# x and mem read a second time with features first; Strassen's sums from the kept normalised x; the first weights in two halves

## The chip, the core and the metric

The kernel runs on one core of a Trainium2 chip. The core's engines run side by side and wait for each other on semaphores: PE (matrix products; PEld is its weight load), DVE and ACT (elementwise work), POOL (here it issues DMAs and little else) and SP (issues DMAs only). The metric is the device time of one execution in microseconds (us), lower is better. A row of the trace such as `PE L143 MATMUL pg<-whi,memh 128*128 128x512 f32` names the engine, the line that recorded the operation, the operation, the tile written and the tiles read, and the shape.

## What is computed

One layer of a decoder trunk over 512 tokens with 2048 features, and 256 memory tokens. The part that the change touches is the entry:

```python
h = rms_norm(x, norm_g)                       # (512, 2048)
proj = h @ w_in                               # 13712 columns: three branches, gates
...
mkv = rms_norm(mem, mem_norm_g) @ w_mem_kv    # (256, 2048) @ (2048, 2048)
ck = rms_norm(mkv[..., :1024].reshape(..., 4, 256), c_k_norm_g)
cv = mkv[..., 1024:].reshape(..., 4, 256)
...
x = x + merged @ w_out
```

`rms_norm(x, g)` divides each token's row by the root of its mean square (plus 1e-6) and multiplies feature by feature with `g`.

## The kernel before, in words

**Products.** PE contracts over the partition axis, so each left operand must lie with features on partitions. All products are float32 made of three passes: each operand is split into a high part (ACT rounds it: `whi`, `memh`, `hh`) and a rest (DVE subtracts: `wlo`, `meml`, `hl`), and PE adds high·high, high·rest and rest·high.

**The stream.** `stream` (line 379) walks through a list of *jobs*. A job of the memory projection is one block of 256 rows by 512 columns of `w_mem_kv` (512 KB): one DMA from SP into a buffer (`wraw`, three of them, or `mraw`, four), one split on ACT, one subtraction on DVE, twelve matmuls (two halves of 128 rows, two blocks of 128 memory tokens, three passes). The projection has four *chunks* of 512 columns with eight jobs each. Chunk `iq0` follows (eight jobs of 24 matmuls), the first one that reads x, and then chunks of 1024 columns by Strassen's algorithm with seven products P1 to P7 of quarter blocks. SP loads weights as buffers come free; up to three jobs are split ahead (`LOOK`).

**The threads.** Side work (normalisation, attention, sums) is written as generators. `run` (line 628) takes steps of them between the jobs' matmuls, by a model of the engines' clocks (`Plan`, line 74) that exists only while the program is written. It settles the order of instructions on each engine; on the chip an engine goes through its own list in that order and stops only where an instruction waits for a semaphore.

**The entry.** `mem_in` is loaded token by token (`px<-mem`, five DMAs on SP between the first weights). `mem_thread` (825) calls `turn_tokens` (784): PE turns blocks of 128 by 128 with a product by the identity (`pa<-ident,px`, 32 of them), ACT and DVE scale by the gain and split from PSUM. The mean squares of mem are taken on ACT, and `mem_rs` scales the chunk's results as they leave PSUM. `x_thread` (840) starts when mem is turned (flag "mem"): eight DMAs of 512 KB on SP (`px<-x`), sums of squares on ACT, a scaling of each row on DVE, 64 turned blocks, and the split into `hh`, `hl`. `small_loads` (709) fetches 13 small tensors by DMAs from POOL; `rotary_tables` (734) follows x.

**The sums for Strassen.** `h_ops_thread` (1659) needs sums and differences of quarters of h. It adds `hh` and `hl` back together (`h_r<-hh,hl`, eight DVE instructions), makes S1, S2, S4 for two groups of features, splits each, and sets "P1 made", which lets the stream prepare the first Strassen weights.

Before the first weights arrive PE multiplies identity tiles in bf16 (`idle`, 703; `WARM = (28, 24)`).

Of the kernel before, what the change touches and what calls it, by code (L numbers as in the profile page):

```python
# [43 lines left out]
def constants():  # L44

    c = np.zeros((P, 33), np.float32)
    c[:, 0] = np.tile(np.asarray(BUCKET_START, np.float32), 4)
    c[:, 1:33] = (10000.0 ** (-np.arange(0, 64, 2) / 64)).astype(np.float32)[None]
    return c

# [226 lines left out]
class Kern:  # L277
# [101 lines left out]
    def stream(self):  # L379
# [33 lines left out]
        def load_some(most):  # L413
            while st["nload"] < len(loads) and most > 0:
# [4 lines left out]
                if l["strassen"] and "strassen pool" not in self.flags:  # L419
                    return  # L420
                pool = dict(wraw=self.wp, sraw=self.gp, so=self.bp, mraw=self.mp)[l["tag"]]
                r = pool.tile([P, 2, 512], F32, name=l["tag"], tag=l["tag"], bufs=size[l["tag"]])
                if isinstance(l["src"], tuple):
# [33 lines left out]
        def halves(jb, src, w, ids=(), now=False):  # L457
            h, l = new_pair()
            h, l = h[:, :, :w], l[:, :, :w]
            nc.scalar.activation(h, src, AF.Copy)  # L460
# [3 lines left out]
            def low():  # L464
                tt(l, src, h, op=OP.subtract)
                done(*ids)
# [4 lines left out]
        def prep(jb):  # L471
# [11 lines left out]
            elif p == "P5":  # L483
                if kb == 0:
                    sh["T2"] = self.gp.tile([P, c["kp"], 512], F32, name="T2", tag="t2")
# [32 lines left out]
        yield "boot"  # L518
# [4 lines left out]
        for ji, jb in enumerate(jobs):  # L523
# [52 lines left out]
            self.backlog = self.CLEAR if jb["last"] and "gates" in self.flags else self.BACKLOG  # L576
# [38 lines left out]
    BOOT = 3  # L615
    WARM = (28, 24)
    REST = 4
    BACKLOG = 4500.0
    CLEAR = 1500.0
    backlog = BACKLOG  # L620
# [7 lines left out]
    def run(self, main, threads):  # L628
# [38 lines left out]
        for r in main:  # L667
            if r == "boot":
                for _ in range(self.BOOT):
                    step(live[0])  # L670
            elif r == "stall":
# [10 lines left out]
    def setup(self):  # L682
# [12 lines left out]
        self.idle(self.WARM[0])  # L695
# [5 lines left out]
        nc.vector.tensor_copy(self.mnegb, self.mneg)  # L701

# [6 lines left out]
    def small_loads(self):  # L709

        nc, A, cp = self.nc, self.A, self.cp
        self.cst = cp.tile([P, 33], F32, name="cst")
        nc.gpsimd.dma_start(self.cst, A["consts"])

        def col(name, src, n):
            t = cp.tile([P, n], F32, name=name)
            nc.gpsimd.dma_start(t, src.rearrange("o (n p) -> p (o n)", p=P),)
            return t

        self.g_x = col("g_x", A["norm_g"], KT)  # L720
        self.g_aq = col("g_aq", A["a_q_norm_g"], 1)
        self.g_ak = col("g_ak", A["a_k_norm_g"], 1)
        self.g_bl = col("g_bl", A["b_q_lat_norm_g"], 4)
        self.g_bk = col("g_bk", A["b_kv_lat_norm_g"], 2)
        self.g_bqn = col("g_bqn", A["b_q_norm_g"][:, :P], 1)
        self.g_bkn = col("g_bkn", A["b_k_norm_g"][:, :P], 1)
        self.g_cq = col("g_cq", A["c_q_norm_g"], 2)
        self.g_ck = col("g_ck", A["c_k_norm_g"], 2)
        self.g_bqr = cp.tile([P, 64], F32, name="g_bqr")
        nc.gpsimd.dma_start(self.g_bqr, A["b_q_norm_g"][:, P:].to_broadcast([P, 64]))  # L730
        self.g_bkr = cp.tile([P, 64], F32, name="g_bkr")
        nc.gpsimd.dma_start(self.g_bkr, A["b_k_norm_g"][:, P:].to_broadcast([P, 64]))

    def rotary_tables(self, pool):

        nc, A, cp = self.nc, self.A, self.cp
        pos = A["positions"]
        pi = pool.tile([P, NT], I32, name="pos_i")
        nc.gpsimd.dma_start(pi, pos.rearrange("o (n p) -> p (o n)", p=P))
        pf = pool.tile([P, NT], F32, name="pos_f")  # L740
        nc.vector.tensor_copy(pf, pi)
# [23 lines left out]
        self.cos = cp.tile([P, NT, 32], F32, name="cos")  # L765
        nc.scalar.activation(self.sin, r, AF.Sin)
        nc.vector.tensor_scalar(k, r, -1.0, None, op0=OP.mult)
        nc.vector.tensor_tensor(k, r, k, op=OP.max)
        nc.vector.tensor_scalar(k, k, -1.0, math.pi / 2, op0=OP.mult, op1=OP.add)
        nc.scalar.activation(self.cos, k, AF.Sin)  # L770
# [13 lines left out]
    def turn_tokens(self, n, src, half, gain, name, boot=False):  # L784
# [3 lines left out]
        per = 4 // n  # L788
        prev = None

        def finish():
            k0, pt = prev
            ks = range(k0, k0 + per)
            ps = [pt[:, k - k0].rearrange("p a b -> p (a b)") for k in ks]
            for k, x in zip(ks, ps):
                nc.scalar.activation(half(k)[0], x, AF.Copy, scale=gain[:, k:k + 1])
            for k, x in zip(ks, ps):
                nc.vector.scalar_tensor_tensor(half(k)[1], x, gain[:, k:k + 1], half(k)[0], op0=OP.mult,
                                               op1=OP.subtract)
                self.flags.add("%s%d" % (name, k))  # L800

        for i, k0 in enumerate(range(0, KT, per)):
            ring = (self.pa, self.pb)[i % 2]
            blocks = [(k, t) + src(t, k) for k in range(k0, k0 + per) for t in range(n)]
            if boot and i > 1:
                yield "job %d" % min(i // 2, 2)
            yield [x[3] for x in blocks] + [ring]
            pt = ring.bank([P, per, n, P])
            for k, t, x, _ in blocks:
                nc.tensor.transpose(pt[:, k - k0, t], x, self.ident)  # L810
            if prev:
                yield [prev[1]]
                finish()
            prev = (k0, pt)
            if boot:
                if i == 0:
                    self.idle(self.WARM[1])
                yield [pt]
                finish()
                prev = None  # L820
        if prev:
            yield [prev[1]]
            finish()

    def mem_thread(self, pool, hi, lo):
        nc = self.nc
        xs = self.mem_in
        yield from self.turn_tokens(2, lambda t, k: (xs[k // 4][:, t, k % 4 * P:(k % 4 + 1) * P], xs[k // 4]),
                                    lambda k: (hi[:, k], lo[:, k]), self.g_m, "mem", True)
        self.flags.add("mem")  # L830
        ss = pool.tile([P, 2], F32, name="m_ss")
        v = pool.tile([P, 2], F32, name="m_v")
        for t in range(2):
            yield from self.sum_squares(pool, [x[:, t] for x in xs], ss[:, t:t + 1])
        yield
        nc.vector.tensor_scalar(v, ss, 1.0 / D, EPS, op0=OP.mult, op1=OP.add)
        self.rsqrt(pool, self.mem_rs, v, 2)
        self.flags.add("mem rs")

    def x_thread(self, pool):  # L840
        nc = self.nc
        src = self.A["x"][0]
        yield "mem"
        xs = []
# [3 lines left out]
        for t in range(NT):  # L848
            xs.append([])
            for q in range(2):  # L850
                x = pool.tile([P, 1024], F32, name="px", tag="px", bufs=8)
                nc.sync.dma_start(x, src[t * P:(t + 1) * P, q * 1024:(q + 1) * 1024])
                xs[t].append(x)
                for _ in range(self.REST):
                    yield
        self.small_loads()
        for t in range(NT):
            yield xs[t]
            yield from self.sum_squares(pool, xs[t], ss[:, t:t + 1])
        yield [ss]  # L860
        nc.vector.tensor_scalar(v, ss, 1.0 / D, EPS, op0=OP.mult, op1=OP.add)
        self.rsqrt(pool, rs, v, NT)
        for t in range(NT):
            for x in xs[t]:
                nc.vector.tensor_scalar(x, x, rs[:, t:t + 1], None, op0=OP.mult)
                yield
        yield from self.turn_tokens(NT, lambda t, k: (xs[t][k // 8][:, k % 8 * P:(k % 8 + 1) * P], xs[t][k // 8]),
                                    self.act_h, self.g_x, "x")
        self.flags.add("x")
        self.rotary_tables(pool)  # L870
# [145 lines left out]
    def c_thread(self):  # L1016
        nc = self.nc
        yield "ipool"
        with self.slots("cpool") as pool:
# [15 lines left out]
            rs_c = pool.tile([P, 4, 6], F32, name="c_rs")  # L1035
            nc.vector.tensor_scalar(vv, self.c_ss, 1.0 / 256, EPS, op0=OP.mult, op1=OP.add)
            self.rsqrt(pool, rs_c.rearrange("p a b -> p (a b)"), vv.rearrange("p a b -> p (a b)"), 24)
            nc.vector.tensor_scalar(rs_c[:, :, :4], rs_c[:, :, :4], C_SCALE, None, op0=OP.mult)
            for h in range(4):
# [34 lines left out]
                yield from self.split_in_turn(vh, vl, v)  # L1074
# [584 lines left out]
    def h_ops_thread(self):  # L1659
# [4 lines left out]
        yield "strassen pool"  # L1664
# [5 lines left out]
        for g in range(2):  # L1670
            ks = slice(4 * g, 4 * g + 4)
            r = self.gp.tile([P, 4, 4, 256], F32, name="h_r", tag="t2")
            blocks = [(j, i) for j in range(2) for i in range(2)]
            for x, (j, i) in enumerate(blocks):
                hi, lo = [y[:, :, 256 * i:256 * i + 256] for y in self.h[2 * j + g]]
                tt(r[:, x], hi, lo, op=OP.add)
                yield [r]
            r11, r21, r12, r22 = [r[:, x] for x in range(4)]
# [3 lines left out]
            yield [r]  # L1682
# [625 lines left out]
```

## Time and profile before

| what | value |
|---|---|
| runs | 1845.24, 1845.20 and 1845.78 us, median 1845.24 us |
| span of the profiled execution, first to last instruction | 1844.1 us |
| between that span and the median of the runs | 1.1 us |
| PE busy | 1831.6 us in 9313 matmuls |
| DVE busy | 1379.0 us |
| ACT busy | 981.5 us |
| POOL busy | 210.0 us |
| moved by DMA | 368.55 MB, 200 GB/s on the mean |

The profile counts an engine as busy while an instruction is in it. Matmuls overlap in the array, so the time that one of them adds to a chain is read from the distance between the starts of neighbours, and not from its own duration. "x24" after a row is a count; "[1.53 <-DMA mraw<-w_mem_kv]" is an idle spell of the engine just before, and what ended it. A window's row gives the busy time of PE, PEld, DVE, ACT and POOL in it, then the granted clock of PE as a share of full speed, the busy share of the 16 DMA engines and GB/s.

### The profile page before, as it was taken

What the parts mean: (1) busy time and instruction counts of PE and PEld (TensorE: products, weight loads), DVE (VectorE), ACT (ScalarE), POOL (GpSimd) and SP (SyncE); (2) the same over time, 40 slices, a digit from 0 to 9 for tenths busy, and PEclk for the clock granted to TensorE, in tenths of its full rate; (3) what the DMA queues carried; (4) which work ended last, traced back from release to release, by engine and by line L of the source; (5) the groups of instructions that cost most, each with busy time, mean ns of one, the idle gap of its engine ahead of it and who ended that gap; (6) DMA issues with size and microseconds to landing.
All of it is one profiled execution on the core that took longest, in us unless ns stands there. A gap on an engine that the chain in (4) does not pass through costs nothing.

```text
span 1844.1 us, 25398 instructions
## 1 busy us (share of the span) xinstructions
PE 1831.6 (99%) x9313; PEld 1533.4 (83%) x9313; DVE 1379.0 (75%) x2118; ACT 981.5 (53%) x1789; POOL 210.0 (11%) x310
## 2 busy tenths in 40 slices
PE   9999999999999999999999999999999999999999
PEld 7887888888888888888889888888878888888787
DVE  6788787777777877778777588999867675667755
ACT  7734544464444444444458866545877942234442
POOL 1000011001010110000112212210112112110000
PEclk9999999999999999999999999999999999999999
DMA  9654596876667967656636634333366467846784
GB/s 344 217 190 136 166 353 186 228 207 182 201 243 254 263 182 206 195 170 194 203 127 220 215 131 137 131 121 119 112 227 210 133 221 260 285 160 206 247 276 139
DMA packets 159756, 368.55 MB, mean 200 GB/s; under 512 B 19072, under 2 KB 27184, under 8 KB 158608
## 3 DMA queue, kind: packets, MB, share of 16 engines
q1 hardware_dynamic: 120592, 232.72, 39.7%
q0 software_dynamic: 39008, 134.21, 22.5%
q8 instruction: 73, 1.20, 0.3%
q14 instruction: 51, 0.42, 0.1%
q10 hardware_dynamic: 32, 0.01, 0.0%
HBM read 308.40 MB, written 92.05 MB: 217 GB/s over the span
## 4 chain that ended last, share of the span: by engine, by line
PE 89%; DVE 6%; ACT 3%; issue 1%; DMA 1%; POOL 0%; SPq 0%; ACTq 0%; DVEq 0%
PE pg L143 55%; PE pn L143 26%; PE pm L143 8%; DVE wlo L143 1%; ACT whi L143 1%; DMA stage<-sp_oC 1%; DVE i_wk L143 1%; DVE i_mx L143 0%; ACT b_pr L143 0%; ACT junk L143 0%; DVE b_st L143 0%; DMA px<-mem 0%; ACT a_st L143 0%; PE pb L143 0%; DVE b_rl L143 0%
## 5 line engine op out<-in xcount | busy, mean ns | idle before, releaser
L143 ACT ACTIVATE whi<-wraw 128x1024 fp32r<-128x1024 f32 (+2 forms) x266 | 277.8, 1047 | 293.1 <-PE pg L143 150.7
L143 DVE TENSOR_TENSOR wlo<-wraw,whi 128x1024 fp32r<-128x1024 f32 (+2 forms) x266 | 321.3, 1209 | 141.2 <-ACT whi L143 140.0
L143 PE MATMUL pg<-whi,u 128*128 128x512 f32 x640 | 216.5, 399 | 0.0
L143 PE MATMUL pg<-hh,whi 128*128 128x512 f32 x448 | 181.7, 406 | 1.0 <-DVE stage L143 1.0
L143 ACT ACTIVATE whi<-sraw 128x1024 fp32r<-128x1024 f32 (+1 forms) x99 | 103.8, 1050 | 134.8 <-DVE sraw L143 59.5
L143 PE MATMUL pg<-hh,wlo 128*128 128x512 f32 x448 | 175.2, 391 | 0.0
L143 PE MATMUL pg<-hl,whi 128*128 128x512 f32 x448 | 174.8, 390 | 0.0
L143 DVE TENSOR_TENSOR wlo<-sraw,whi 128x1024 fp32r<-128x1024 f32 (+1 forms) x99 | 119.9, 1213 | 56.6 <-ACT whi L143 55.7
L143 PE MATMUL pg<-whi,hS 128*128 128x512 f32 (+1 forms) x480 | 156.8, 388 | 0.0
L143 PE MATMUL pn<-whi,hS 128*128 128x512 f32 (+1 forms) x480 | 156.3, 386 | 0.0
L143 PEld LDWEIGHTS pg<-whi,u 128*128 128x128 f32 x640 | 120.2, 188 | 23.2
L143 PE MATMUL pg<-wlo,u 128*128 128x512 f32 x320 | 124.9, 390 | 0.0
L143 PE MATMUL pg<-whi,hl 128*128 128x512 f32 (+1 forms) x320 | 124.0, 388 | 0.0
L143 PE MATMUL pn<-whi,hl 128*128 128x512 f32 (+1 forms) x320 | 124.0, 388 | 0.0
L143 PE MATMUL pg<-wlo,hh 128*128 128x512 f32 (+1 forms) x320 | 123.9, 387 | 0.0
L143 PE MATMUL pn<-wlo,hh 128*128 128x512 f32 (+1 forms) x320 | 123.9, 387 | 0.0
L143 PE MATMUL pn<-whi,hh 128*128 128x512 f32 (+1 forms) x320 | 123.7, 387 | 0.0
L143 PE MATMUL pg<-whi,hh 128*128 128x512 f32 (+1 forms) x320 | 123.7, 387 | 0.0
L143 DVE TENSOR_TENSOR wlo<-T,whi 128x1024 fp32r<-128x1024 f32 (+1 forms) x80 | 96.7, 1209 | 31.3 <-ACT whi L143 31.1
L143 ACT ACTIVATE whi<-T 128x1024 fp32r<-128x1024 f32 (+1 forms) x80 | 84.0, 1050 | 67.7 <-PE pn L143 25.9
L143 PEld LDWEIGHTS pg<-whi,hS 128*128 128x128 f32 x480 | 90.1, 188 | 18.0
L143 PEld LDWEIGHTS pn<-whi,hS 128*128 128x128 f32 x480 | 90.1, 188 | 17.3
(452 smaller groups left out, 4112.7 us busy)
## 6 DMA issues: line engine op xcount, KB each, us to landing
wraw<-w_in SPq DMA_DIRECT2D x146, 512.0 KB, 3.9
sraw<-w_in SPq DMA_DIRECT2D x90, 512.0 KB, 4.3
wT<-w_out POOLq DMA_DIRECT2D x24, 1024.0 KB, 21.4
wraw<-w_branch SPq DMA_DIRECT2D x48, 512.0 KB, 4.7
yg<-sp_g POOLq DMA_DIRECT2D x24, 512.0 KB, 5.3
wraw<-wT SPq DMA_DIRECT2D x19, 512.0 KB, 4.0
mraw<-w_mem_kv SPq DMA_DIRECT2D x17, 512.0 KB, 6.9
wT<-wT POOLq DMA_DIRECT2D x8, 1024.0 KB, 12.7
```

Source lines behind the costliest of these rows:

```text
L143: return f(*a, **k)
```

## The change

Two inputs more are given to the kernel, `xT` and `memT`: x and mem with features first (2048 by 512, 2048 by 256). The small parameters arrive in one array `cols` of 191 columns, and `g_m` by itself.

```diff
+    def x_loads(self):
+        nc = self.nc
+        yield "mem2"
+        src = self.A["x"][0]
+        self.rows = [self.hp[n // 2].tile([P, D], F32, name="row%d" % t, tag="h%s%d" % (x, n)) ...]
+        pieces = [("row%d %d" % (t, h), self.rows[t][:, h * 1024:(h + 1) * 1024], src[t * P:(t + 1) * P, ...])
+                  for t in range(NT) for h in range(2)]
+        pieces += [("xs%d" % k, self.xs[k // 4][:, k % 4:k % 4 + 2], self.A["xT"][k * P:(k + 2) * P]...)
+                   for k in range(0, KT, 2)]
+        for name, a, b in pieces:
+            nc.gpsimd.dma_start(a, b)
+            self.flags.add(name)
+            for _ in range(self.REST):
+                yield
...
     def mem_thread(self, pool, hi, lo):
-        yield from self.turn_tokens(2, ..., self.g_m, "mem", True)
+        for i in range(KT // 2):
+            ...
+            for k, x, g in ks:
+                nc.scalar.activation(hi[k // 2][:, k % 2], x, AF.Copy, scale=g)
+            for k, x, g in ks:
+                nc.vector.scalar_tensor_tensor(lo[k // 2][:, k % 2], x, g, hi[k // 2][:, k % 2], ...)
...
     def x_thread(self, pool):
-                nc.sync.dma_start(x, src[t * P:(t + 1) * P, q * 1024:(q + 1) * 1024])
...
-            for x in xs[t]:
-                nc.vector.tensor_scalar(x, x, rs[:, t:t + 1], None, op0=OP.mult)
-        yield from self.turn_tokens(NT, ..., self.act_h, self.g_x, "x")
+        nc.vector.tensor_copy(wide, bc(rs, [P, NT, P], 2))
+        for t in range(NT):
+            nc.tensor.transpose(pt[:, t * P:(t + 1) * P], wide[:, t], self.ident)
+        nc.scalar.activation(rb, pt, AF.Copy)
+        for i in range(KT // 2):
+            for a in range(2):
+                nc.vector.scalar_tensor_tensor(x[:, a], x[:, a], self.g_x[...], rb, op0=OP.mult, op1=OP.mult)
+            self.split(hh, hl, x)
...
     def h_ops_thread(self):
-                tt(r[:, x], hi, lo, op=OP.add)
-            r11, r21, r12, r22 = [r[:, x] for x in range(4)]
+            r11, r21, r12, r22 = [self.xs[2 * j + g][:, :, 256 * i:256 * i + 256] for j in range(2) for i in range(2)]
...
-                if g and n == "S1":
+                if g and n == "S2":
                     self.flags.add("P1 made")
+        self.more_gates()
...
         def load_some(most):
-                if l["strassen"] and "strassen pool" not in self.flags:
+                if l["tag"] == "sraw" and "strassen pool" not in self.flags:
+                if isinstance(l["src"], tuple) and not st["nload"]:
+                    (w,), row = l["src"]
+                    for k in range(2):
+                        nc.sync.dma_start(r[:, k], w[row + k * P:row + k * P + P, :])
+                        self.second_load()
...
-    WARM = (28, 24)
+    WARM = 36
+    FIRST = 8000.0
...
         def mem_load(a, b):
-            q = a // 512
-            load(self.mem_in[q][:, :, a - q * 512:b - q * 512], src[:, :, a:b])
+            q = a // 4
+            load(self.mem_in[q][:, a - 4 * q:b - 4 * q], src[:, a:b])
```

So mem comes with features on partitions, in pieces of 1, 1, 2, 2, 2, 4 and 4 feature blocks; no block of it is turned. Its squares are summed over features by ACT and DVE (`mem_stats`, new: four squares, three adds, four small products by a column of ones on PE), and `mem_rs` is now applied to the keys' norms and to the values in `c_thread`. x is read twice, by rows for its sums of squares and with features first for the work. The factor 1/rms of each token is spread over all partitions by four turned blocks (`x_rb`), and x is scaled in place and kept, which gives `h_ops_thread` its quarters. The tiles `xs` make room for the weights `sraw` only when these sums are made (`more_gates`). `rotary_tables` runs later, in the Strassen stage. The first job's weights are loaded and split in two halves.

On POOL, at the start of the program, up to the first evacuated result of the memory projection. Before (`sp_ck0` is that result, the rest are small parameters):

```order
L686 IOTA jp_90 128x128
L143 DMA sp_ck0_153<-stage_526 128x1024 [waits DVE_49,Activation_49]
L143 DMA cst_615<-consts 128x33
L143 DMA g_x_617<-norm_g 128x16x1
L143 DMA g_aq_619<-a_q_norm_g 128x1
```

And now (`row` is x by tokens, `xs` x by features; a wait named DMASW is for a DMA that POOL itself issued earlier):

```order
L711 IOTA jp_90 128x128
L157 DMA row0_260<-x 128x1024 x2
L157 DMA row1_261<-x 128x1024 x2
L157 DMA cols_303<-cols 128x191
L157 DMA row2_262<-x 128x1024 x2
L157 DMA row3_263<-x 128x1024
L157 DMA row3_263<-x 128x1024 [waits DMASW0_49]
L157 DMA xs0_160<-xT 128x2x512 [waits DMASW1_49]
L157 DMA xs0_160<-xT 128x2x512 [waits DMASW2_49]
L157 DMA sp_ck0_180<-stage_462 128x1024 [waits DMASW3_49,DVE_49,Activation_49]
```

Eight halves of x's rows and two pieces of `xs`, ten DMAs of 512 KB, stand ahead of `sp_ck0`, and none of them waits for SP, PE, ACT or DVE.

On SP, the first loads. Before (`px` is mem, `wraw` and `mraw` weights):

```order
L143 DMA px_192<-mem 128x2x256
L143 DMA wraw_198<-w_mem_kv 128x2x512
L143 DMA px_192<-mem 128x2x256
L143 DMA wraw_201<-w_mem_kv 128x2x512
L143 DMA px_193<-mem 128x2x512
L143 DMA wraw_204<-w_mem_kv 128x2x512
L143 DMA px_194<-mem 128x2x512
```

And now:

```order
L157 DMA mem0_150<-memT 128x256
L157 DMA wraw_220<-w_mem_kv 128x512
L157 DMA mem0_150<-memT 128x256
L157 DMA wraw_220<-w_mem_kv 128x512
L157 DMA mem0_150<-memT 128x2x256
L157 DMA wraw_225<-w_mem_kv 128x2x512
L157 DMA mem1_151<-memT 128x2x256
L157 DMA wraw_228<-w_mem_kv 128x2x512 [waits DMAHW0_49]
```

The same bytes in smaller first pieces; the eight loads of x that stood on SP further down have gone to POOL.

On DVE, at the end of `iq0` and the start of the first Strassen chunk. Before (`hS` are the split sums, `stage` takes iq0's result out of PSUM, `T2` and `wraw<-wraw` are sums of weights):

```order
L143 TENSOR_TENSOR hS2_1242<-h_r_1374,hS2_1242 128x1024 [waits Activation_49]
L143 TENSOR_TENSOR h_r_1374<-h_r_1374 128x1024
L143 TENSOR_TENSOR hS4_1243<-h_r_1374,hS4_1243 128x1024 [waits Activation_49]
L143 COPY stage_1483<-pg_1216 128x512 [waits DMASW0_49,PE_49]
L143 COPY stage_1501<-pg_1218 128x512 [waits DMASW5_49,PE_49]
L143 TENSOR_TENSOR T2_1511<-wraw_1386,wraw_1316 128x1024 [waits DMAHW0_49,DVE_49]
L143 TENSOR_TENSOR wraw_1349<-wraw_1386,wraw_1349 128x1024
L143 TENSOR_TENSOR wlo_1514<-wraw_1316,whi_1513 128x1024 [waits Activation_49]
```

And now:

```order
L157 TENSOR_TENSOR hS4_1130<-xs3_163,hS4_1130 128x1024 [waits Activation_49]
L157 TENSOR_TENSOR wlo_1290<-wraw_1156,whi_1289 128x1024 [waits DMAHW1_49,PE_49,Activation_49]
L157 TENSOR_TENSOR wraw_1156<-wraw_1192,wraw_1156 128x1024 [waits DMAHW2_49,DVE_49]
L157 TENSOR_TENSOR T2_1294<-wraw_1227,wraw_1156 128x1024 [waits DMAHW3_49,DVE_49]
L157 TENSOR_TENSOR wlo_1297<-wraw_1156,whi_1296 128x1024 [waits PE_49,Activation_49]
L157 TENSOR_TENSOR wraw_1192<-wraw_1227,wraw_1192 128x1024
L157 TENSOR_TENSOR wlo_1328<-T2_1294,whi_1327 128x1024 [waits PE_49,Activation_49]
L157 COPY stage_1337<-pg_1055 128x512 [waits DMASW2_49,PE_49]
```

The weights of the first three Strassen products are prepared ahead of the copies that wait for the end of `iq0`, where `T2` stood behind them.

More of the change, by code (lines that the diff above doesn't have):

```diff
@@ L49, in constants, with column, row @@
     return c
+COLUMNS = (("cst", 33), ("g_x", KT), ("g_aq", 1), ("g_ak", 1), ("g_bl", 4), ("g_bk", 2), ("g_bqn", 1), ("g_bkn", 1),
+           ("g_cq", 2), ("g_ck", 2), ("g_bqr", 64), ("g_bkr", 64))
+def column(g):
+    return np.asarray(g).reshape(-1, P).T
+def row(g):
+    return np.broadcast_to(np.asarray(g).reshape(1, -1), (P, np.asarray(g).size))
 LINE = 128
@@ L614 @@
     GAP = 3
-    BOOT = 3
-    WARM = (28, 24)
+    WARM = 36
     REST = 4
@@ L665, in force, with boot @@
             step(live[i])
[L667 to L671, printed above, removed]
+        def boot(n=1):
+            for _ in range(n):
+                step(live[0])
+        for r in main(boot):
+            if r == "stall":
                 force()
@@ L711, in small_loads, with rotary_tables @@
         nc, A, cp = self.nc, self.A, self.cp
[L712 to L734, printed above, removed]
+        n = sum(w for _, w in COLUMNS)
+        cols = cp.tile([P, n], F32, name="cols")
+        nc.gpsimd.dma_start(cols, A["cols"])
+        c0 = 0
+        for name, w in COLUMNS:
+            setattr(self, name, cols[:, c0:c0 + w])
+            c0 += w
+    def rotary_tables(self):
         nc, A, cp = self.nc, self.A, self.cp
+        yield "strassen 5"
+        pool = self.gp2
         pos = A["positions"]
@@ new lines, in mem_thread, with mem_stats @@
+        self.flags.add("mem")
+    def mem_stats(self, pool):
+        nc = self.nc
+        xs = self.mem_in
+        yield "mem"
+        yield "row1 squared"
+        acc, sq = [self.hp[0].tile([P, 8, NM], F32, name="m_" + n, tag=tag)[:, :4] for n, tag in (("acc", "hh1"), ("sq", "hl1"))]
+        for q in range(4):
+            nc.scalar.activation(sq if q else acc, xs[q][:, :4], AF.Square)
+            yield
+            if q:
+                yield [sq]
+                nc.vector.tensor_tensor(acc, acc, sq, op=OP.add)
+        self.flags.add("mem squared")
+        yield
+        nc.vector.tensor_tensor(acc[:, :2], acc[:, :2], acc[:, 2:], op=OP.add)
+        nc.vector.tensor_tensor(acc[:, 0], acc[:, 0], acc[:, 1], op=OP.add)
+        ah = pool.tile([P, NM], F32R, name="m_ah")
+        al = pool.tile([P, NM], F32R, name="m_al")
+        yield [acc]
+        self.split(ah, al, acc[:, 0])
+        yield [al, self.pa]
+        pt = self.pa.bank([P, 2, 4])
+        for t in range(2):
+            for a in (ah, al):
+                nc.tensor.matmul(pt[:, t], a[:, t * P:(t + 1) * P], self.ones, start=a is ah, stop=a is al)
@@ L848, in x_thread @@
         for t in range(NT):
-            xs.append([])
-            for q in range(2):
-                x = pool.tile([P, 1024], F32, name="px", tag="px", bufs=8)
-                nc.sync.dma_start(x, src[t * P:(t + 1) * P, q * 1024:(q + 1) * 1024])
[L853 to L859, printed above, removed]
+            row = self.rows[t]
+            yield "row%d 1" % t
+            yield [row]
+            yield from self.sum_squares(pool, [row[:, :1024], row[:, 1024:]], ss[:, t:t + 1])
+            self.flags.add("row%d squared" % t)
         yield [ss]
@@ L1035, in c_thread @@
             rs_c = pool.tile([P, 4, 6], F32, name="c_rs")
+            scale = bc(self.mem_rs, [P, 4, 2], 1)
+            for _ in range(2):
+                nc.vector.tensor_tensor(self.c_ss[:, :, 4:], self.c_ss[:, :, 4:], scale, op=OP.mult)
             nc.vector.tensor_scalar(vv, self.c_ss, 1.0 / 256, EPS, op0=OP.mult, op1=OP.add)
@@ L1073, in c_thread @@
                 vl = pool.tile([P, 2, 256], F32R, name="c_vl", tag="c_vl")
-                yield from self.split_in_turn(vh, vl, v)
+                for t in range(2):
+                    yield from self.split_in_turn(vh[:, t], vl[:, t], v[:, t], self.mem_rs[:, t:t + 1])
                 self.c_v = vh, vl
@@ L2194, in build @@
                     for j in range(2 if c < 2 else 0)]
-            self.chunk(wm[:, c * 512:(c + 1) * 512], KT, 512, lambda k: (memh[:, k], meml[:, k]), "tm", 2,
-                       self.to_dram(key, 2, 512, lambda: self.mem_rs, sums), lambda k: ("mem%d" % (k + 1), "mem rs" if k == 14 else None))
+            self.chunk(wm[:, c * 512:(c + 1) * 512], KT, 512, lambda k: (memh[k // 2][:, k % 2], meml[k // 2][:, k % 2]), "tm", 2,
+                       self.to_dram(key, 2, 512, sums=sums), lambda k: "mem%d" % (k + 1))
             self.chunks[-1]["early"] = True
@@ L2267, in first @@
         def first():
-            mem_load(0, 256)
-            self.nc.scalar.dma_start(g_rows, A["mem_norm_g"].rearrange("o (n p) -> (o n) p", p=P))
-        def gains():
-            pt = self.pb.bank([P, KT])
-            self.nc.tensor.transpose(pt, g_rows, self.ident[:KT, :KT])
-            self.nc.scalar.activation(self.g_m, pt, AF.Copy)
-        self.first_loads = [first, lambda: mem_load(256, 512), lambda: mem_load(512, 1024),
-                            lambda: mem_load(1024, 1536), lambda: mem_load(1536, 2048), gains]
@@ new lines, in build @@
+        pieces = [(1, 2)]
+        self.second_load = lambda: pieces and mem_load(*pieces.pop())
+        self.first_loads = [first] + [lambda a=a, b=b: mem_load(a, b)
+                                      for a, b in ((2, 4), (4, 6), (6, 8), (8, 12), (12, 16))]
+        self.run(self.stream, [
+            self.mem_thread(sp, memh, meml), self.x_loads(), self.x_thread(sp), self.mem_stats(sp), self.rotary_tables(), self.latent_thread(), self.kpe_thread(), self.c_thread(), self.c_part(0), self.c_part(1), self.b_part(0), self.b_part(1), self.b_part(2), self.b_thread(), self.a_thread(0), self.a_thread(1), self.a_bias_thread(apre, kpool), self.idx_thread(apre, kpool), self.h_ops_thread(), self.t_thread(), self.u_thread(), close_h()])
@@ L2299 @@
     arrays = {name: np.ascontiguousarray(inputs[name]) for name in _INS}
-    arrays["consts"] = constants()
+    arrays["xT"] = np.ascontiguousarray(np.asarray(inputs["x"])[0].T)
+    arrays["memT"] = np.ascontiguousarray(np.asarray(inputs["mem"])[0].T)
+    arrays["g_m"] = np.ascontiguousarray(column(inputs["mem_norm_g"]))
+    bq, bk = [np.asarray(inputs[n])[0] for n in ("b_q_norm_g", "b_k_norm_g")]
+    arrays["cols"] = np.ascontiguousarray(np.concatenate([constants()] + [
+        column(inputs[n]) for n in ("norm_g", "a_q_norm_g", "a_k_norm_g", "b_q_lat_norm_g", "b_kv_lat_norm_g")] + [
+        column(bq[:P]), column(bk[:P]), column(inputs["c_q_norm_g"]), column(inputs["c_k_norm_g"]),
+        row(bq[P:]), row(bk[P:])], axis=1))
     A = {name: nc.dram_tensor(name, a.shape, mybir.dt.from_np(a.dtype), kind="ExternalInput").ap()
```

163 lines of the change are left out of this document (81 added, 82 removed).

## The prediction

> **What bounds the kernel now.** The page's head, its busy times, the chain that ended last and the granted clock come first.
>
> ```profile
> span 1844.1 us, 25398 instructions
> PE 1831.6 (99%) x9313; PEld 1533.4 (83%) x9313; DVE 1379.0 (75%) x2118; ACT 981.5 (53%) x1789; POOL 210.0 (11%) x310
> PE 89%; DVE 6%; ACT 3%; issue 1%; DMA 1%; POOL 0%; SPq 0%; ACTq 0%; DVEq 0%
> PEclk9999999999999999999999999999999999999999
> ```
>
> PE is busy for 99% of the span at full clock, so time changes in two ways only: PE gets fewer or more instructions, or PE stands still somewhere. The table of windows says where it stands still.
>
> ```profile
> core 0: us, PE busy (x) PEld busy (x) DVE busy (x) ACT busy (x) POOL busy (x), PEclk, DMA share, GB/s
> 0.00:10.00 10.00, 7.60 (x68) 6.66 (x69) 3.13 (x10) 4.53 (x9) 0.42 (x5) 1.00 0.79 261
> 10.00:20.00 10.00, 9.63 (x56) 7.74 (x54) 7.15 (x11) 6.63 (x12) 0.00 (x0) 1.00 1.05 388
> 34.00:150.00 116.00, 116.00 (x545) 96.45 (x544) 90.17 (x118) 65.26 (x94) 14.06 (x22) 1.00 0.61 201
> 150.00:160.00 10.00, 8.76 (x39) 6.91 (x39) 9.95 (x10) 5.17 (x6) 0.98 (x2) 1.00 0.75 262
> ```
>
> Between 34 and 150 us PE has no gap, while DVE has 26 us and DMA 39% to spare: whatever leaves PE's list there is gained in full. From 10 to 20 us the DMA engines are full (1.05, 388 GB/s): what is loaded more there delays what stands beside it. Near 152 us there is a small hole. The chain of waits gives the prices.
>
> ```profile
> 20.21 53.75 PE pg L143 x237
> 73.97 0.44 PE pa L143 x4
> ...
> 96.47 0.44 PE pb L143 x4
> 96.91 53.09 PE pg L143 x234
> 150.05 0.57 issue
> 150.63 1.21 DVE T L143
> 151.84 1.14 DVE wraw L143
> 152.98 1.15 DVE wlo L143
> ```
>
> One matmul of 128x512 adds 53.75 / 237 = **0.2268 us**, so a job of the memory projection (12) takes 2.72 us and one of `iq0` (24) 5.44. The span is 1844.1, the median of the runs 1845.24: 1.14 us lie outside the span and are added at the end.
>
> **A. The turned blocks of x go.** The first and the last of 16 groups of four transposes stand in that chain, 0.44 us each, in PE's gapless stretch: 16 x 0.44 = **-7.0 us**. That PE does the rest without a gap needs x in time. `iq0` has eight jobs, 43.5 us, and ends near 150, so it starts near 106. The last pieces of `xs` stand on POOL behind the store of the first result, near 45 us at the latest by term B; 3.1 MB at 388 GB/s are 8 us, the work on x on DVE 22 us (next rows): some 20 us remain.
>
> ```profile
> L143 DVE TENSOR_TENSOR wlo<-mraw,whi 128x1024 fp32r<-128x1024 f32 x17 | 20.8, 1222 | 5.8 <-ACT whi L143 5.0 <-DMA wraw<-w_mem_kv 0.7
> L143 DVE TENSOR_TENSOR h_r<-hh,hl 128x1024 f32<-128x1024 f32 x8 | 9.5, 1219 | 0.0
> L143 DVE SCALAR_TENSOR_TENSOR hl<-pa,g_x,hh 128x512 fp32r<-128x512 f32 x8 | 6.0, 747 | 1.9 <-ACT hh L143 1.8
> L143 DVE TENSOR_SCALAR px<-px,x_rs 128x1024 f32<-128x1024 f32 x8 | 5.7, 746 | 0.0
> L143 ACT ACTIVATE whi<-mraw 128x1024 fp32r<-128x1024 f32 x17 | 17.8, 1058 | 5.9 <-PE pg L143 4.2 <-DMA mraw<-w_mem_kv 1.5
> L143 ACT ACTIVATE memh<-pa,g_m 128x256 fp32r<-128x256 f32 x8 | 3.3, 473 | 0.5 <-PE pa L143 0.5
> ```
>
> DVE loses 9.5 (`h_r`), 5.7 (`px`) and 16 x 0.747 = 12.0 (`hl`): 27.2 us. It gains 16 scalings of 128x512 at 0.747 = 12.0, eight subtractions of 128x1024 at 1.22 = 9.8, and some 4.6 for the squares of mem (three adds at 1.22, the rest small): 26.4 us. So DVE's 90 of 116 us stay, and I cost the elementwise part at 0; its cover is those 26 us, and beyond them each 2.72 us too late holds PE by one memory job.
>
> **B. The start: x beside the first weights.** These rows show how the start goes now.
>
> ```profile
> 7.44 0.50 PE L143 MATMUL pg<-whi,memh 128*128 128x512 f32 x1 [0.60 <-ACT whi L143]
> 17.67 1.06 ACT L143 ACTIVATE whi<-mraw 128x1024 fp32r<-128x1024 f32 x1 [1.53 <-DMA mraw<-w_mem_kv]
> 19.97 0.48 PE L143 MATMUL pg<-whi,memh 128*128 128x512 f32 x1
> 23.92 0.46 SPq L143 DMA_DIRECT2D px<-x  x1
> ```
>
> The last wait of ACT for a weight ends at 17.67, and x is first read at 23.92, behind the weights that matter. Job 3 starts at 19.97, job 5 two jobs later at 25.41, and PE has no gap any more. Now POOL issues ten DMAs of 512 KB (5.24 MB of x) and `cols` with no wait for another engine, so from the first microseconds. How two queues share the engines is seen where POOL and SP load together, between 257 and 262 us:
>
> ```profile
> DMA packets 658, 1.88 MB, mean 376 GB/s; under 512 B 44, under 2 KB 44, under 8 KB 658
> q0 software_dynamic: 329, 1.25, 64.0%
> q1 hardware_dynamic: 329, 0.63, 37.4%
> ```
>
> The number of packets is the same, 329 and 329: **the queues take turns, packet by packet**, and POOL's packets (3.8 KB on the mean) are twice SP's (1.9 KB). One POOL packet holds an engine for 0.640 x 16 x 5 us / 329 = 0.156 us. Ten DMAs in rows of 4 KB are 1280 packets, 80 on each engine: 12.5 us, and `cols` (98 KB) 0.25 more. SP must bring mem (2.10 MB, 1-KB rows) and six weight blocks (3.15 MB, 2-KB rows) ahead of job 5, which is 128 + 96 = 224 packets on an engine. Taking turns, all 80 of POOL's are through before SP's 224: job 5's weights are later by the whole **12.75 us**.
>
> What slack stands against it? The row at 17.67 is the split of the fifth block, so 4.72 MB had landed; the sixth block takes 0.524 / 0.388 = 1.35 us more: 19.0, or 20.3 if mem's rows, now of 1 KB where they were up to 2 KB, cost as much once more. Then four `memh` (0.473), `whi` (1.06) and `wlo` (1.22) make 4.2 us: 23.2 to 24.5 without x, against 25.41 now. Slack 0.9 to 2.2, taken 1.5. The first term is therefore **+11.25 us**. Its ends are -2.2 (x does not get in the way, all slack is won) and 13.5 - 0.9 = +12.6 (5.24 MB at 388 GB/s). I stay at the upper part, since the row of equal packet counts is the only one of two loading queues. The first weights in halves and the eight groups of turned mem blocks are inside this term: they shorten the time before job 1, but not the landing of the sixth block.
>
> The Trainium skill, "DMA: Bandwidth & Descriptors", section "Queues, rings and completion order", says that each engine goes round the queues at packet granularity and drains a whole packet of typically 9 to 17 descriptors before it switches. The turn-taking agrees with the rows; the size does not, since SP's packets are of 1.9 KB there. With such packets on SP's side alone x would hardly be felt; that is rival 2.
>
> **C. The hole at Strassen's start.**
>
> ```profile
> 154.16 0.50 PE L143 MATMUL pg<-wlo,hS 128*128 128x512 f32 x1 [1.24 <-DVE wlo L143]
> 156.95 5.44 PE pn L143 x24
> ```
>
> PE waits 1.24 us for `wlo`, the end of a row of DVE work (`T`, `wraw`, `wlo` in the chain above). DVE is freed of 9.5 us of `h_r` just ahead, and the first three products' weights now stand ahead of the copies at `iq0`'s end: **-1.24 us** (0 to -1.24). Next late would be `sraw`, loaded only once the sums are made: eight sums and six splits, 14 x 1.22 = 17 us, with eight jobs' `wlo`, 10 us, inside 43.5 us. 16 us remain for the load.
>
> **D. What PE gets.** Four transposes for the row factors, one group: **+0.44**. Four products of 128x4 by ones are not in the trace; nearest is the small transpose here, from its start to the next one's start.
>
> ```profile
> 4.62 0.28 PE L143 MATMUL pb<-ident,g_rows 16*128 16x16 f32 x1
> 4.83 0.68 PE L143 MATMUL pa<-ident,px 128*128 128x128 f32 x4
> ```
>
> That is 0.21 us, four are **+0.8** (0 to 4 x 0.2268 = 0.9). The tables of angles, moved into Strassen's stage, the small products with `mem_rs` and the changed order of later threads I take as 0 with 2 us to either side: PE's idle time after 160 us is small, as 1831.6 of 1844.1 shows.
>
> **Sum:** 11.25 - 7.04 - 1.24 + 0.44 + 0.8 = **+4.2**: span 1848.3, run 1849.5 us.
>
> **Rivals.**
>
> 1. *Not slower: x does not take the start.* If POOL's first data come only when SP has the first six blocks, term B is 0 to -1.5 and the sum -7.0 to -8.5: 1836.7 to 1838.2 us. For it speaks POOL's first DMA now:
>
> ```profile
> 36.85 0.69 POOL L143 DMA_DIRECT2D sp_ck<-stage  x1 [35.78 <-ACT junk L143]
> 45.38 0.55 POOL L143 DMA_DIRECT2D g_bkn<-b_k_norm_g  x1 [3.03 <-DMA sp_ck<-stage]
> ```
>
> It took 8.5 us from issue to landing. Against it: a delay of 8 us still leaves x landing from about 10 us on, in the fullest window. It decides from the point where x's first packet comes after 17 us. Chance 0.14.
>
> 2. *SP keeps most of the engines.* If one turn of SP moved nine rows of 2 KB against one of 4 KB, POOL would move 5.24 x 4/18 = 1.16 MB before job 5, 3.0 us, less slack 1.5: +1.5 in place of 11.25, run 1839.7 us. The equal packet counts speak against it. The Trainium skill's rule named above gives this. Chance 0.06.
>
> 3. *A part of x only.* If POOL starts 4 to 8 us late, or PE's jobs of before are split sooner so that slack is larger, term B is +5 to +8: 1843.2 to 1846.2 us. Chance 0.24.
>
> 4. *The clock falls in the new waits.* PE now waits before jobs 1 to 5, 11 us together. If the last wait is long enough for the clock to be halved, about one job of 2.72 us is run twice as long: 1852.2. All granted clocks in the rows are 1.00, with idle spells up to 1 us only. The Trainium skill, "TensorE: Matmul & The Clock Gate", section "What's actually happening", gives about 3.4 us of idleness for the fall to half; no row here shows it. Chance 0.06.
>
> That PE would still turn x's blocks is ruled out by the lists of instructions: four transposes are left.
>
> **How the numbers follow.** The forecast has 0.50, with an own range of 1847.3 (POOL one microsecond or two late) to 1851.0 (upper end of B). A measurement of this kernel can tell about 0.2%, 3.7 us, from no change, which is 1841.5 to 1848.9; 0.05 of the forecast lies inside. Faster: rivals 1 and 2 and a little of 3, 0.21. Same: most of 3 and that part, 0.28. Slower: the rest, 0.51. Both signs hold much, so the range goes from rival 1 to rival 4: 1837.0 to 1852.5.
>
> **What would show it.** B: packets of x in the first 10 us, as many in POOL's queue as in SP's up to 28 us, waits of PE for `whi` or `wlo` of jobs 1 to 5 that end with a DMA of weights, job 5 near 36.5 in place of 25.4, the first chunk's end near 45. A: no transposes of `px` between 70 and 100 us and no gap of PE there. C: the first Strassen product without a wait. D: four short products in the memory projection. Wrong would be B if job 5 starts before 30 us; A if PE waits at `iq0`'s start for `hh` or `hl`; the zero of the rest if PE's idle time after 160 us grows by over 2 us.

## The result, and the profile after

| | before | after |
|---|---|---|
| median of the runs | 1845.22 us (4 runs, 1844.97 to 1845.78) | 1865.50 us (4 runs, 1864.55 to 1866.48) |
| span of the profiled execution | 1844.1 us | 1864.2 us |

The change makes the kernel slower: the ratio is 1.0110, with a 95% interval of 1.0096 to 1.0125. The sign is as forecast, the size is not: 1849.5 us were forecast, and the range ended at 1852.5. The page's head of the changed kernel:

```profile
span 1864.2 us, 25175 instructions
PE 1841.2 (99%) x9208; PEld 1529.6 (82%) x9208; DVE 1380.0 (74%) x2124; ACT 981.9 (53%) x1775; POOL 212.1 (11%) x315
PEclk8999999999999999999999999999999999999999
```

PE has 105 matmul records fewer and is yet busy for 9.6 us longer (1841.2 against 1831.6). Standing still is therefore only about half of the 20.1 us of span; in the rest PE works, but slower. The table of windows shows the start, with the columns that it had before:

```profile
0.00:10.00 10.00, 5.85 (x41) 5.00 (x42) 3.23 (x11) 3.76 (x6) 5.72 (x15) 0.98 0.80 255
10.00:20.00 10.00, 5.96 (x14) 3.90 (x14) 2.11 (x3) 1.96 (x3) 1.03 (x2) 0.67 1.03 398
20.00:30.00 10.00, 5.71 (x14) 3.81 (x13) 4.04 (x6) 4.23 (x7) 0.00 (x0) 0.67 1.06 373
30.00:40.00 10.00, 10.00 (x38) 8.07 (x38) 7.90 (x13) 7.86 (x13) 0.00 (x0) 0.83 1.05 386
```

DMA is full from 10 to 40 us, PE makes 14 matmuls in each of two stretches of 10 us, and the granted clock is 0.67 there. PE's timeline in the changed kernel has the waits behind it, in brackets, and the step at half clock:

```profile
8.86 1.07 PE L157 MATMUL pg<-whi,memh 128*128 128x512 f32 x3 [2.47 <-ACT whi L157]
...
16.80 0.80 PE L157 MATMUL pg<-whi,memh 128*128 128x512 f32 x1 [3.58 <-ACT whi L157]
...
27.92 0.80 PE L157 MATMUL pg<-wlo,memh 128*128 128x512 f32 x1 [3.25 <-DVE wlo L157]
28.51 0.63 PE L157 MATMUL pg<-whi,meml 128*128 128x512 f32 x1
28.94 0.63 PE L157 MATMUL pg<-whi,memh 128*128 128x512 f32 x1
...
33.78 0.39 PE L157 MATMUL pg<-whi,memh 128*128 128x512 f32 x1
34.01 0.40 PE L157 MATMUL pg<-wlo,memh 128*128 128x512 f32 x1
```

From 27.92 us on PE has no gap; up to 33 us its step is 0.43 us, then 0.23. PE's timeline before has the first product that reads x here:

```profile
106.30 0.39 PE L143 MATMUL pg<-hh,whi 128*128 128x512 f32 x1
```

And in the changed kernel:

```profile
112.97 0.39 PE L157 MATMUL pg<-hh,whi 128*128 128x512 f32 x1
```

So 6.67 us are lost at the entry to `iq0`, of which the forecast had 11.25 - 7.04 + 1.24 = 5.45. **The entry came out nearly as forecast; some 13 us more are lost behind it**, where the forecast had a gain of 1.24 (term C) and 0 for all the rest. The chain of waits shows one source, in the stretch of the attention branch:

```profile
1391.39 1.73 ACT a_st L157 x6
1393.12 0.21 issue
1393.34 2.73 ACT a_st L157 x9
1396.07 0.95 ACT u L157
1397.02 0.02 issue
1397.04 1.24 DVE u L157
```

The window around it, with the columns as above:

```profile
1390.00:1402.00 12.00, 8.61 (x75) 6.72 (x74) 6.05 (x13) 11.49 (x34) 1.28 (x3) 0.87 0.95 322
```

ACT rounds a piece of `u` (an operand of the products that PE is at) only behind a row of comparisons `a_st`; PE stands still for 2.87 us meanwhile and then has a lower clock (0.87). The other source is in no list of waits. The chain has a group of twelve Strassen matmuls, one kind of product on one block of weights; before:

```profile
646.59 2.72 PE pg L143 x12
```

Now it is:

```profile
655.12 2.75 PE pg L157 x12
```

0.03 us in 2.72 look like nothing. But between the first product with hS (160.57 us, 152.54 before) and the end there are some 6000 matmuls of this shape, and PE has hardly a gap: 2 ns more in each are 12 us.

### The profile page after: what moved, and what is told of

Read it like the earlier page. It is cut to its first block, busy times and chain, and to the rows that moved or that the text cites. A ratio compares the mean times of both kernels' runs of the same rounds, so it can differ in the third digit from the quotient of the medians.

```text
span 1864.2 us, 25175 instructions
## 1 busy us (share of the span) xinstructions
PE 1841.2 (99%) x9208; PEld 1529.6 (82%) x9208; DVE 1380.0 (74%) x2124; ACT 981.9 (53%) x1775; POOL 212.1 (11%) x315
## 4 chain that ended last, share of the span: by engine, by line
PE 92%; ACT 3%; DVE 2%; DMA 1%; issue 1%; SPq 0%; ACTq 0%; DVEq 0%
PE pg L157 58%; PE pn L157 25%; PE pm L157 9%; DMA mem<-memT 1%; ACT whi L157 1%; ACT junk L157 1%; DVE wlo L157 1%; ACT a_st L157 0%; DMA sp_oC<-c_pr 0%; DVE m L157 0%; SPq L157 0%; DVE mask L157 0%; DVE u L157 0%; ACT b_pr L157 0%; ACT stage L157 0%
## 5 line engine op out<-in xcount | busy, mean ns | idle before, releaser
L157 ACT ACTIVATE whi<-wraw 128x1024 fp32r<-128x1024 f32 (+3 forms) x267 | 278.2, 1044 | 321.1 <-PE pg L157 156.8
L157 DVE TENSOR_TENSOR wlo<-wraw,whi 128x1024 fp32r<-128x1024 f32 (+3 forms) x267 | 321.6, 1206 | 133.1 <-ACT whi L157 131.9
```

What stands on the lines that cost most here:

```text
L157: return f(*a, **k)
```

## The experiments

**Where do longer steps come from?** From the starts of neighbouring matmuls, over all 576 of a kind in Strassen's chunks (864 with hS): `wlo` by `hh` takes 226.8 ns before and 231.7 now, `whi` by `hh` 226.9 and 229.2, `whi` by `hl` 226.3 and 226.0, `whi` by `hS` 226.7 and 226.6. SBUF is the memory that holds the tiles; the kernel lays its pools from both ends of it, left and right. The products that got longer have one operand on the left side (weights) and the other on the right (h, later a part of u), though not all such products did: `whi` by `hl` did not. With hS both lie on the left. The pool `cp`, the first on the left, holds the small parameters; it shrank from 5376 to 4672 bytes per partition, and all that stands behind it on the left moved by 704 bytes, five and a half times 128. `cp` has a spare tile named `rest`, and the right side one named `edge`, which set these places.

*e1_line:*

```diff
-        cp.tile([P, 24], F32, name="rest")
+        cp.tile([P, 8], F32, name="rest")
```

> The changed kernel with the spare tile `rest` of pool cp at 8 columns in place of 24, so that every tile on the left side of SBUF (weights and their halves) starts at a multiple of 128 bytes, as before the change; in the changed kernel they start 64 bytes behind one. The order of instructions is the same on every engine. Theory L (PE's step with hh, 0.2317 us for wlo x hh against 0.2268 before, comes from the place of the two operands in a line of 128 bytes): these steps go back to 0.2268 and the run takes 12 us less, near 1853.5 us. Rival D (the steps are longer because of what runs beside them, DMA or other engines, or because of the chip): nothing changes, near 1865.5 us.

Measured: 1854.84 us (4 runs), 10.7 below the changed kernel, and the group of twelve is back:

```profile
651.51 2.72 PE pg L157 x12
```

Over half of the loss is the place of tiles in memory. The mean clock (0.994) stays, and nearly so the first product with x:

```profile
112.77 0.39 PE L157 MATMUL pg<-hh,whi 128*128 128x512 f32 x1
```

*e2_before_off* (the same diff in the kernel before) and *e3_edge* (in the changed kernel):

```diff
-        edge.tile([P, (LINE - 32) // 4], F32, name="edge")
+        edge.tile([P, (LINE - 32 + 64) // 4], F32, name="edge")
```

> The kernel before with `rest` at 8 columns in place of 24, so that its weights start 64 bytes behind a multiple of 128, as in the changed kernel; nothing else. Theory L: wlo x hh goes from 0.2268 to about 0.2317 us, the run to 1855 to 1858 us. Rival D: 1845.2 us, steps as before.

> The changed kernel with the tile `edge` 64 bytes longer, so that the right side of SBUF (h, u, xs) starts 64 bytes behind a multiple of 128 too, as the weights do. If what counts is that both operands lie alike in a line (theory L, first form): steps back to 0.2268, near 1853.5 us. If each operand must start at a multiple of 128 by itself (theory L, second form): no gain or a loss, 1865 us or more. Rival D: 1865.5 us.

Measured: 1865.65 us for e2, about twice the loss that was expected (ratio 1.0113, interval 1.0096 to 1.0130), and 1877.17 us for e3, 22.3 more than e1. Rival D is out: a kernel whose order, DMA and work are those of before loses 20 us. The group of twelve in the chain of e2:

```profile
654.24 2.80 PE pg L143 x12
```

In e3:

```profile
658.71 2.79 PE pg L157 x12
```

But e3 fell on the side of "each operand by itself", and in e2 the weights lie on the same remainder of 128 as in the changed kernel and cost 20 us, twice what e1 takes off that one. So four more places were tried in the kernel before: *e5_before_edge* (`edge` as in e3), *e6_before_32* (`rest` at 16), *e9_before_both* (`rest` at 8 and `edge` as in e3) and *e10_before_128* (`rest` at 56).

> The kernel before with `edge` 64 bytes longer: h and u on the right side of SBUF start 64 bytes behind a multiple of 128, the weights on the left side stay on one. Theory L, second form (each operand must start on a line of 128 bytes by itself): products of weights with hh, hl and u get 2 to 6 ns longer, those of weights with hS (both on the left) stay at 226.6 ns, and the run takes 1853 to 1866 us. Rival W (only the place of the weights counts): 1845.4 us.

> The kernel before with `rest` at 16 columns in place of 24: the weights start 96 bytes behind a multiple of 128, 32 bytes short of the next. Theory L, second form: as slow as with 64 bytes, 1855 to 1866 us, products with hh near 233 ns. Rival H (only the half line counts, or multiples of 32 are as good): 1845.4 us.

> The kernel before with `rest` at 8 columns and `edge` 64 bytes longer: weights and h both start 64 bytes behind a multiple of 128, and alike within 256 bytes (in e3_edge they lay 128 apart within 256). If only the distance between the two operands counts: products with hh at 226.9 ns, 1845 us. If each must start on a line of 128 bytes: 230 to 233 ns, 1855 us or more.

> The kernel before with `rest` at 56 columns in place of 24: the weights start on a multiple of 128 as before, but 128 bytes on, so that weights and h lie 128 apart within 256. If multiples of 128 are enough: steps of 226.9 ns, 1845 us. If the distance within 256 counts: products with hh near 230 to 233 ns, 1855 us or more.

The place of the weights and of h within 256 bytes, and what was measured (steps from the starts of neighbours, as above; the last three rows have the new order of work, and are to be compared with each other):

| kernel | weights | h | weights minus h | whi x hh, wlo x hh, ns | us |
|---|---|---|---|---|---|
| before | 128 | 128 | 0 | 226.9, 226.8 | 1845.2 |
| e9 | 64 | 64 | 0 | 226.7, 226.6 | 1845.32 |
| e5 | 128 | 64 | 64 | 229.2, 231.7 | 1855.24 |
| e10 | 0 | 128 | 128 | 233.3, 232.5 | 1865.87 |
| e2 | 64 | 128 | 192 | 233.3, 233.3 | 1865.65 |
| e6 | 96 | 128 | 224 | 232.8, 233.0 | 1867.49 |
| changed kernel | 192 | 128 | 64 | 229.2, 231.7 | 1865.50 |
| e1 | 128 | 128 | 0 | 226.7, 226.9 | 1854.84 |
| e3 | 192 | 64 | 128 | 233.3, 232.5 | 1877.17 |

e5 came out as the second form expected, e6 1.5 us above its range, and rivals W and H, which had 1845.4 us, are out. e9 against e10 decides. e9 has neither operand on a multiple of 128, and its ratio is 1.0002 (0.9992 to 1.0011); e10 has both on one, and its ratio is 1.0112 (1.0098 to 1.0126). The group of twelve in e9:

```profile
646.38 2.72 PE pg L143 x12
```

And in e10:

```profile
654.32 2.79 PE pg L143 x12
```

What counts is how the two operands of a matmul lie **to each other**, not where each of them lies. Both forms that I had taken from multiples of 128 are wrong, and the prices too: 64 off costs 10 us, 128, 192 and 224 cost 20 to 23. In bytes the weights of e1 lie 768 lower against h than those of before, at the same steps, so the pattern may repeat after 256 bytes or another divisor of 768; 256 is the smallest that fits these rows. One thing does not fit: at 128, 192 and 224 the products of `whi` by `hS`, which moved together, are longer too, by 1.1 to 1.5 ns (e6, e10, e3 and e2). That, what inside the chip makes it so, and distances that were not tried stay open.

**The start.** *e4_line_sp* is e1 with x loaded by SP, behind the first weights:

```diff
     def x_loads(self):
-        yield "mem2"
+        yield "mem"
...
-            nc.gpsimd.dma_start(a, b)
+            nc.sync.dma_start(a, b)
```

> As e1_line, and x's sixteen loads (rows and features first) are issued by SP behind the first memory jobs' weights, as the eight loads of x were before, and no longer by POOL at the start. Theory S (the start is late because x takes turns with mem and the first weights, and the clock falls in the waits): PE has no wait over 1 us after the first job, the half clock is gone from the start, the eighth memory job ends near 33 us as before, and the run is some 12 to 14 us below e1_line, near 1840 us. Rival (the new form of the start, mem by features and the halves, is slow by itself): the start stays late, within 3 us of e1_line.

Measured: 1842.96 us (10 runs), 11.9 below e1, and a little below the kernel before (ratio 0.9987, 0.9978 to 0.9996). The windows of e4 from 0 to 30 us:

```profile
0.00:10.00 10.00, 6.66 (x46) 5.80 (x47) 3.87 (x13) 4.67 (x8) 1.11 (x6) 1.00 0.75 230
10.00:20.00 10.00, 7.65 (x32) 5.43 (x31) 6.47 (x11) 7.44 (x13) 0.00 (x0) 1.00 1.06 373
20.00:30.00 10.00, 10.00 (x46) 8.29 (x45) 8.88 (x11) 6.45 (x9) 0.00 (x0) 1.00 1.05 390
```

From 10 us on the engines of DMA are as full as in the changed kernel, but with weights: from 20 us on PE has no gap and a full clock. The first product with x is here:

```profile
99.05 0.39 PE L157 MATMUL pg<-hh,whi 128*128 128x512 f32 x1
```

That is 7.25 us earlier than before and 13.7 earlier than in e1; the run keeps 11.9 of these, since the hole of 1.24 us at Strassen's start is back (below). PE still waits 1.8 us inside the first job; behind it no wait at the start is over 1 us, as expected. Who had the engines in the changed kernel is seen in its DMA queues from 10 to 20 us:

```profile
DMA packets 1567, 3.98 MB, mean 398 GB/s; under 512 B 146, under 2 KB 457, under 8 KB 1567
q0 software_dynamic: 782, 2.77, 70.1%
q1 hardware_dynamic: 785, 1.21, 32.9%
```

782 packets of POOL and 785 of SP: they take turns, and POOL's, of 3.5 KB on the mean, are over twice as large as SP's (1.5). In these 10 us the running count of one queue drifts against the other's within a band of 12 packets, on 16 engines, so a turn is one packet or very few; most are single rows, of 4 KB from POOL and of 1 or 2 KB from SP. The rule on packets of 9 to 17 descriptors (the Trainium skill, "DMA: Bandwidth & Descriptors", section "Queues, rings and completion order") is right here about the turns and not about the size.

*e7_warm* is e1 with PE kept at work in these waits (in `stream`, `fill` multiplies identity tiles):

```diff
+                        if x == 0 and (kk, b) == order[0]:
+                            self.fill(56)
...
+            if ji in (1, 2):
+                self.fill(40 if ji == 1 else 24)
...
+                    if ji == 2 and (kk, b) == order[0]:
+                        self.fill(40)
```

> e1_line with 160 products of identity tiles put into PE's waits in the first three memory jobs (56, 40, 24 and 40 of them); the order of all else is the same. Theory C (the waits let the clock fall, and the matmuls behind the last wait run at half clock for 5 us: 13 of them at 0.427 in place of 0.227 us, 2.6 us): the granted clock stays at 1.00 up to 40 us, the end of the start is set by the landing of the weights at the same 28 us, and the run is 2 to 3 us below e1_line, near 1852.3 us. Rival (the half clock lies under the waits for data and costs nothing): 1854.8 us.

Measured: 1853.90 us, 0.9 below e1 and between the two expectations, with the first product with x at 111.58 us against 112.77. The two runs are of different rounds, in which the kernel before took 1844.80 and 1845.41 us, so the trace's 1.2 us is the better measure. The clock did not stay full all the time, as the windows of e7 from 10 to 40 us show:

```profile
10.00:20.00 10.00, 6.21 (x54) 4.99 (x55) 2.84 (x5) 2.59 (x4) 1.45 (x2) 0.97 1.04 402
20.00:30.00 10.00, 9.38 (x83) 7.67 (x82) 4.04 (x6) 3.82 (x6) 0.00 (x0) 0.86 1.06 372
30.00:40.00 10.00, 9.69 (x43) 7.65 (x42) 8.37 (x13) 8.17 (x13) 0.00 (x0) 1.00 1.05 385
```

From 30 us on it is full, where it was 0.85 in e1; but PE, now faster, loses 0.31 us there in a new wait, and the gapless part began at 28.44 instead of 27.95. So of the 2.6 us at half clock behind the last wait about 1.2 could be won here; the later begin (0.5) and the new wait (0.31) took most of the rest.

**The wait for u.** *e8_u* is e4 with this edit in `gate`:

```diff
+        if n == 2 and k == 3:
+            self.nc.vector.tensor_copy(u[:, 0], o)
+            self.nc.vector.tensor_tensor(u[:, 1], o, u[:, 0], op=OP.subtract)
+        else:
+            self.split(u[:, 0], u[:, 1], o)
```

> e4_line_sp with the high part of the fourth piece of u of the first branch made by DVE (a copy) in place of ACT, where it stands behind nine comparisons a_st; PE waits 2.91 us for it there and then runs 6.8 us at half clock. Theory U (this wait and its half clock are the 5 us that the changed kernels lose between 1350 and 1400 us): PE has no wait over 1.5 us there, the clock stays at 1.00, and the run takes 4 to 6 us less than e4_line_sp, near 1838 us. Rival (another wait comes up behind it, since ACT and DVE are full there): within 2 us of e4_line_sp.

Measured: 1839.01 us (6 runs), 3.95 below e4, ratio 0.9968 to before (0.9956 to 0.9979). The window from 1370 to 1382 us in e4:

```profile
1370.00:1382.00 12.00, 9.05 (x72) 6.88 (x71) 5.54 (x14) 11.13 (x34) 0.00 (x0) 0.72 0.87 307
```

And in e8:

```profile
1370.00:1382.00 12.00, 11.12 (x93) 8.73 (x92) 10.03 (x24) 10.72 (x36) 0.73 (x2) 1.00 0.96 335
```

PE's wait for `u` in e4:

```profile
1375.55 0.80 PE L157 MATMUL pg<-whi,u 128*128 128x512 f32 x1 [2.91 <-ACT u L157]
```

And in e8:

```profile
1373.24 0.50 PE L157 MATMUL pg<-whi,u 128*128 128x512 f32 x1 [0.35 <-DVE u L157]
```

The clock is full again and the wait is 0.35 us in place of 2.91. Theory U holds for the wait and the clock; its price is just under the 4 to 6 us expected, and 3.3 us if e8 and e4 are each taken against the kernel before of their own round (1844.80 and 1845.41 us). The half clock was longer in e4 (0.72 over 12 us) than in the changed kernel (0.87), so part of the gain may be a loss of e4's own.

**The hole at Strassen's start.** In the changed kernel PE goes through it without a wait, as forecast; in e4 and e8 the 1.24 us are back. *e11_x_earlier* is e8 with `yield "mem8"` in place of `yield "mem"` in `x_loads`.

> e8_u with x's loads on SP begun two weights earlier, when half of mem is split. Theory H (PE's hole at Strassen's start is closed only if the sums of x end before the copies at the end of iq0, which is a matter of when x lands; in e4 and e8 it lands too late and the 1.24 us are back): the hole goes, the start stays as in e8 (first product with hh near 99 us), and the run is 1 to 1.5 us below e8, near 1837.8 us. Rival (x earlier takes from the first weights again): the start is 2 us or more later and nothing is won, 1839 us or more.

Measured: **1837.57 us** (5 runs, 1837.14 to 1837.82), ratio 0.9958 (0.9945 to 0.9970), 1.4 below e8 (2.1 if each is taken against the kernel before of its own round). The chain through the start of Strassen's part in e8 goes over DVE:

```profile
143.51 1.22 DVE T L157
144.72 1.13 DVE wraw L157
145.86 1.15 DVE wlo L157
```

In e11 it stays on PE:

```profile
94.94 53.34 PE pg L157 x234
148.27 5.44 PE pn L157 x24
```

In e8 the last sum of x (`hS`, 140.44 us on DVE) runs just ahead of the two copies of `iq0`'s result, and `T` comes only behind the copies, at 143.51; in e11 the sums of x are done at 137, and `T` (139.59) runs ahead of the copies (144.14), as in the changed kernel. The first product with x is at 98.85 us: x two weights earlier cost the start nothing. e11 is the fastest kernel here, 7.9 us below the one before.

## Why the prediction was wrong

The steps of e1, e4, e8 and e11 lead from 1865.50 to 1837.57: 10.7 for the place of the tiles, 11.9 for the start with its clock, 3.95 for the wait for `u`, 1.4 for the hole. The last two compare runs of different rounds and are uncertain by some 0.7 us; and the hole is a loss that e4 brought back. The loss of the changed kernel itself, 20.3 us, is 6.67 at the entry, less 1.24 at Strassen's start, 10.7 for the place of the tiles, and some 4.2 that are left, for which the wait for `u` is the only piece found. The sign was no luck: the terms that were forecast came to 6.67 - 1.24 = +5.4 in place of +4.2, which alone would have been 1850.7 us.

- **The step that failed is the sum's "rest", taken as 0 with 2 us to either side: it keeps every matmul behind the entry at the duration of before.** One matmul was 0.2268 us throughout. The change to the small parameters, which I had costed only as one DMA in place of 13, moved the weights against h by 64 bytes within 256, `wlo` by `hh` went from 226.8 to 231.7 ns, and e1 shows the price: 10.7 us. No view of the profile of before could show it, but the diff does: the sizes in `cp` change, and next to them stands a spare tile whose only use is to set a place.
- **The zero for the order of later threads was wrong too.** 2.9 us of waiting for `u` and half a clock behind it: e8 takes away 3.95 us. The sign that I had named came: PE's idle spells after 160 us add up to 4.2 us before and to 6.5 now. I took the small idle time of before as the measure; but the planner makes such an order anew with every change, and ACT is busy for 11.49 of 12 us there. Which part of the change made this wait was not tried.
- **B, the start: right in its mechanism, too small.** One packet of POOL for one of SP, x ahead of the first weights, the late start: all as written. Job 5 starts at 38.57 us, against 25.52 before and 36.5 forecast. The term was +11.25; measured, from the first product with x, 6.67 + 7.04 - 0.78 = 12.9. Rival 4, the clock, came true beside it and not in place of it; I had given the two as cases that exclude each other. (That the rows held idle spells up to 1 us only was a misreading: the one at 154.16 has 1.24, at full clock.) Its price of 2.72 us was about right for the matmuls at half clock (13 by 0.2 us), but in e7 only 1.2 of it could be won.
- **Rival 1's size is borne out by e4:** without x in the way the start is 7.25 - 7.04 + 0.78 = 1.0 us earlier than before, inside its 0 to 1.5.
- **A was right:** PE turns no block of x and has no gap from 28 us to Strassen's part (rows below). **C was right** in the changed kernel, on a condition that I had not named: e8 and e11 show that x must land soon enough. **D** was 0.78 in place of 1.24: 0.44 for the four turned blocks, and 0.34 for the four small products, which I had at 0.8. The chain of the changed kernel has them both, and goes on without a wait into Strassen's part:

```profile
74.77 0.44 PE pb L157 x4
...
86.79 0.34 PE pa L157 x4
87.13 76.35 PE pg L157 x330
163.47 5.47 PE pn L157 x24
```

## What to carry to other kernels

An edit that changes the size of a small tile can move every large one behind it: compare where the operands of the busiest instruction lie before and after, and look at the step of one and the same group of instructions in both profiles before looking for waits. A queue with large packets that starts without a wait takes the DMA engines from whatever is needed first; put such loads in the queue of what they must not overtake. Where PE waits long, look for a half clock behind the wait, and do not treat the two as alternatives; how much of it counts depends on what PE would wait for next.

## What the runs showed of the hardware

- A matmul of 128x512 in float32 (`whi` and `wlo` by `hh`) takes 226.6 to 226.9 ns when its two operands lie alike within 256 bytes (before, e1, e9), and 229.2 to 233.3 ns at distances of 64, 128, 192 and 224 bytes. A kernel of some 6700 matmuls of this shape, not all of them with operands on both sides, lost 10 to 23 us of 1845. At a distance of 64 the price is not the same for all: `whi` by `hl` stays at 226.
- The clock fell to half in or behind waits of PE of 2.5 to 3.9 us (changed kernel, e1, e4), and behind two close together, of 2.07 and 0.76 us in e7 and of 2.32 and 0.76 in e1; not behind the 1.8 us of e4 (1.00 in its windows). The Trainium skill, "TensorE: Matmul & The Clock Gate", section "What's actually happening", gives about 3.4 us of idleness in windows that run free of the program; the 2.91 us before `u` in e4 were enough for a clock of 0.72 over 12 us.
